# RWKV-7 recurrence in a two-layer decoder: a tile's two heads as row halves, products that alternate among the array's quarters, the inverse one turn a step

## The chip, the cores and the metric

One core of one Trainium2 chip runs the whole program. The metric is the time of one execution on the device, in microseconds (us). TensorE (PE) multiplies, VectorE (DVE), ScalarE (ACT) and GpSimd (POOL) work on tiles, SyncE (SP) and POOL issue the DMA transfers.

## What is computed

A trunk of two layers on 256 tokens of width 2048 in float32: a gated linear recurrence (RG-LRU) with its MLP, then an RWKV-7 time mixing with its MLP. The change touches only the time mixing. Cut to what matters:

```python
def rwkv7_time_mix(x, ...):
    r, k, v = ...                      # three 2048x2048 projections of shifted x
    decay, a, g = ...                  # low-rank projections
    kk = heads(k * k_k); kk = kk / max(norm(kk), 1e-12)      # 32 heads of 64
    k_mod = k * (1.0 + (a - 1.0) * k_a)
    def step(state, inp):              # state: 64x64 for each head
        r_t, w_t, k_t, v_t, kk_t, a_t = inp
        sa = einsum('bhij,bhj->bhi', state, kk_t)
        state = (state * w_t[:, :, None, :]
                 - sa[..., None] * (kk_t * a_t)[:, :, None, :]
                 + v_t[..., None] * k_t[:, :, None, :])
        y_t = einsum('bhij,bhj->bhi', state, r_t)
        return state, y_t
    _, y = lax.scan(step, state0, xs)
    y = group_norm(y) * ln_g + ln_b + bonus(r, k_mod, v)
    return (y * g) @ w_out
```

## The kernel before, in words

**Tiles.** The 256 tokens are four chunks (c = 0 to 3) of T = 64. The 2048 features are 16 tiles of 128 partitions, and one tile f holds two heads (e = 0, 1) of 64. Two tiles make a pair p (0 to 7), eight tiles a half hf (0, 1), four tiles a group s of a half. The scan over tokens is rewritten by chunks: inside a chunk a 64x64 triangular matrix of each head and chunk is inverted, and from chunk to chunk a 64x64 state is carried.

**Projections.** `linear` (from L196) streams a weight matrix in chunks of 128x1024 (`raw`). ACT casts a chunk to `hi` (L153), DVE subtracts to get `lo` (L154), two chunks ahead (AHEAD = 2). PE then multiplies each 128x128 block three times (`mm3`, L189 to L191). After every fourth k it calls `between`, which steps generators ("lanes") at a rate given per projection, so that the recurrence's work is mixed into the stream of the projections k, r, v and rwo (the output projection; PSUM tiles `ps_k`, `ps_r`, `ps_v`, `ps_rwo`). A scheduler then sets the order on each engine from these steps, with some reordering by readiness. In the profile k runs until about 1155 us, r from 1155 to 1300, v from 1300 to 1473, rwo from 1473 to about 1632.

**Preparation.** Lane `prep` (L686) runs once a tile while r and v are multiplied: low-rank products `pu`, squared norms `pn` (L725, 4 matmuls of 2 columns a tile), a scan for the decays, the tiles `BK` and `ZR` (L742 to L749), the products of all pairs of tokens of a chunk `sc`, their mask (`SC`, L766), and transposes of BK into `BKT`. Then POOL stores SC, ZR and BKT to scratch in DRAM (`scD` L772, `zrD` L773, `bkD` L777) with 1, 1 and half a transfer a tile; it also stores and reloads the pair's r (`rD` L783, `rs` L680). All of these stand on POOL's queue in the order of the program.

**Inverse.** Lane `diag`: `diagonal(hf)` (L801) loads the 32x32 diagonal blocks of the triangles of eight tiles from scD, and inverts 128 x 8 of them at once on DVE, row by row: 31 turns of a multiplication (L832) and an addition (L836) of up to 128x256 elements. It yields twice a turn for half 0 and once for half 1. `inverse(hf)` (L845) transposes the result on DVE (L854 XD, L856 XR) and makes the off-diagonal block in 32x32 products on PE: `pq` (L870), a copy to `G` on ACT, `px` (L876), a copy into `XT`; first for one row half (bh = 0), then for the other.

**Core.** Lanes core0 and core1: `core(hf, s)` (L929) goes through the four chunks for the four tiles of its group. With each chunk it makes `pw` = old state times Z (L973) plus the triangle's upper part times V (L977), scales it to `Ws` on DVE (L981), `pu` = inverse times Ws (L988), copies it to `U` on ACT, then `pS` (L997) for the new state `Sb` (DVE L1001, L1003), and y in the other row half of pw (L1007), which ACT copies out (L1011). The two row halves of a tile of tokens are two chunks: with chunk parity `par`, V lies in the rows of its parity (`pk`) and Ws and U in the other rows (`pb`), so that L997 and L1007 contract V and U in one matmul of 128 rows. The state Sb is a 128x128 block diagonal of two heads, so L973 is a 128x128 matmul. All eight matmuls of a step of L977, and of L988, lie in the same quarter of the array:

```python
            for f, e, o in es:                                   # L976
                pe.matmul(
                    pw[pb, f, o], lhsT=SC[pk, f, e, zo : zo + T], rhs=VU[pk, f, o],
                    start=c == 0 and f + e == 0, stop=True, skip_group_check=True,
                )
```

**Around it.** `centred` makes V without its mean (`pc`, L917, 4 matmuls of 128x128 a pair), `output` turns Y back with 4 transposes a pair (`pyt`, L1048) and adds the bonus and gate. Every fp32 matmul stands twice in the records, as two instructions.

## Time and profile before

| | |
|---|---|
| median of 3 runs | 2364.64 us (2361.79 to 2365.59) |
| the profiled execution | 2363.43 us |
| its span, first to last instruction | 2361.7 us |
| mean granted TensorE clock | 0.990 of 2.4 GHz |
| busy, share of the span | PE 98%, PE's weight loads 89%, DVE 66%, ACT 52%, POOL 5% |

The profile is one execution. The times of its rows are added up against 2363.43 us; the median of the runs is 1.2 us above. Busy PE time is not useful work by itself: matmuls overlap, so what a matmul costs is read from the distance of starts within a run of like ones, not from its length. A row of the timeline that says x32 is a run of 32 instructions, with the time from the first start to the last end.

### The profile page before, as it was taken

The numbers are of one execution on the slowest core, as the hardware profiler recorded it, in microseconds if no ns is written. First come the engines' busy times: TensorE is split into PE (matmuls) and PEld (weight loads), VectorE is DVE, ScalarE is ACT, GpSimd is POOL, SyncE is SP. The second block draws the span as 40 slices with busy tenths as digits, with TensorE's granted clock in tenths as the row PEclk, the third lists the DMA queues.
The fourth block names the chain that finished last, engine by engine and source line by source line (L and its number), as shares of the span: only waits on it lengthen the run. The fifth ranks groups of instructions, "written<-read, shape, count | busy, mean of one in ns | idle before, by whom it ended". The sixth has DMA issues, their size and how long they took to land.

```text
span 2361.7 us, 39553 instructions
## 1 busy us (share of the span) xinstructions
PE 2317.3 (98%) x16040; PEld 2095.0 (89%) x16040; DVE 1563.8 (66%) x2024; ACT 1236.2 (52%) x1664; POOL 119.7 (5%) x218
## 2 busy tenths in 40 slices
PE   8999999999999999989999999999999999999998
PEld 8999888888888888879989899998888888888887
DVE  7777666666656666678788948467666566666565
ACT  7787544444444444568676544345444444444454
POOL 0000000000000000000023231200000000000000
PEclk9999999999999999989999999899999999999999
DMA  6655655555565565655678877645656655655654
GB/s 225 194 167 170 191 183 189 189 190 190 188 188 189 187 194 188 205 170 197 205 252 278 281 240 244 203 148 181 190 190 188 188 189 190 190 188 188 188 187 143
DMA packets 132135, 463.12 MB, mean 196 GB/s; under 512 B 15728, under 2 KB 15984, under 8 KB 131952
## 3 DMA queue, kind: packets, MB, share of 16 engines
q1 hardware_dynamic: 115568, 405.54, 53.9%
q0 software_dynamic: 15808, 52.96, 7.0%
q8 instruction: 125, 2.05, 0.4%
q10 hardware_dynamic: 576, 2.10, 0.2%
q14 instruction: 58, 0.48, 0.1%
HBM read 430.13 MB, written 30.41 MB: 195 GB/s over the span
## 4 chain that ended last, share of the span: by engine, by line
PE 89%; DVE 3%; DMA 2%; issue 2%; ACT 2%; POOL 1%; SPq 0%; ACTq 0%; POOLq 0%; DVEq 0%
PE ps_up L234 20%; PE ps_dn L234 20%; PE ps_up L236 10%; PE ps_dn L236 10%; PE ps_rgout L234 2%; PE ps_rwo L234 1%; PE ps_gate L191 1%; PE ps_gate L190 1%; PE ps_gate L189 1%; PE ps_k L191 1%; PE ps_k L190 1%; PE ps_k L189 1%; PE ps_rgout L236 1%; PE ps_rec L191 1%; PE ps_rec L190 1%
## 5 line engine op out<-in xcount | busy, mean ns | idle before, releaser
L154 DVE TENSOR_TENSOR lo<-raw,hi 128x1024 fp32r<-128x1024 f32 x736 | 900.2, 1224 | 660.9 <-ACT hi L153 660.1
L153 ACT CAST hi<-raw 128x1024 fp32r<-128x1024 f32 x736 | 772.7, 1050 | 942.8 <-PE ps_dn L234 365.5
L234 PE MATMUL ps_up<-mx,hi 128*128 128x512 f32 x2048 | 644.3, 396 | 0.0
L234 PE MATMUL ps_dn<-ao,hi 128*128 128x512 f32 x1984 | 623.5, 396 | 0.0
L236 PEld LDWEIGHTS ps_up<-mx,lo 128*128 128x128 f32 x2048 | 384.7, 188 | 90.9
L236 PEld LDWEIGHTS ps_dn<-ao,lo 128*128 128x128 f32 x1984 | 372.7, 188 | 88.1
L236 PE MATMUL ps_up<-mx,lo 128*128 128x256 f32 x2048 | 402.4, 278 | 0.0
L236 PE MATMUL ps_dn<-ao,lo 128*128 128x256 f32 x1984 | 389.8, 278 | 0.0
L234 PEld LDWEIGHTS ps_up<-mx,hi 128*128 128x128 f32 x2048 | 312.1, 189 | 0.2
L234 PEld LDWEIGHTS ps_dn<-ao,hi 128*128 128x128 f32 x1984 | 302.0, 189 | 0.0
L189 PE MATMUL ps_rec<-rgx,hi 128*128 128x256 f32 x256 | 73.8, 288 | 8.7 <-ACT hi L153 8.7
L234 PE MATMUL ps_rgout<-rgy,hi 128*128 128x512 f32 x256 | 80.4, 396 | 0.6 <-ACT hi L153 0.6
L189 PE MATMUL ps_k<-xk,hi 128*128 128x256 f32 x256 | 74.4, 291 | 4.3 <-ACT xk L153 3.0
L191 PE MATMUL ps_k<-xk,lo 128*128 128x256 f32 x256 | 74.3, 291 | 2.6 <-DVE lo L154 2.6
L191 PE MATMUL ps_v<-xv,lo 128*128 128x256 f32 x256 | 73.8, 288 | 2.2 <-DVE lo L154 2.2
L189 PE MATMUL ps_v<-xv,hi 128*128 128x256 f32 x256 | 74.9, 292 | 0.0
L191 PE MATMUL ps_rec<-rgx,lo 128*128 128x256 f32 x256 | 73.9, 289 | 1.0 <-DVE lo L154 1.0
L190 PE MATMUL ps_k<-xk,hi 128*128 128x256 f32 x256 | 74.3, 290 | 0.4 <-DVE xk L154 0.4
L190 PE MATMUL ps_v<-xv,hi 128*128 128x256 f32 x256 | 73.8, 288 | 0.0
L190 PE MATMUL ps_rec<-rgx,hi 128*128 128x256 f32 x256 | 73.8, 288 | 0.0
L189 PE MATMUL ps_r<-xr,hi 128*128 128x256 f32 x256 | 73.5, 287 | 0.0
L191 PE MATMUL ps_r<-xr,lo 128*128 128x256 f32 x256 | 72.9, 285 | 0.0
(336 smaller groups left out, 3552.0 us busy)
## 6 DMA issues: line engine op xcount, KB each, us to landing
raw<-in_up SPq DMA_DIRECT2D x256, 512.0 KB, 3.9
raw<-in_down SPq DMA_DIRECT2D x256, 512.0 KB, 3.8
raw<-in_rkv SPq DMA_DIRECT2D x96, 512.0 KB, 4.6
raw<-in_w_in SPq DMA_DIRECT2D x64, 512.0 KB, 4.3
raw<-in_rg_out SPq DMA_DIRECT2D x32, 512.0 KB, 3.6
raw<-in_rw_out SPq DMA_DIRECT2D x32, 512.0 KB, 3.7
scD<-SC POOLq DMA_DIRECT2D x16, 512.0 KB, 5.9
SCc<-scD POOLq DMA_DIRECT2D x16, 512.0 KB, 6.8
```

The source lines that it names most:

```text
L153: nc.scalar.copy(out=hi, in_=src)
L154: dve.tensor_tensor(out=lo, in0=src, in1=hi.bitcast(F32), op=ALU.subtract)
L189: pe.matmul(ps, lhsT=whi, rhs=xhl[:, 0:S], start=start, stop=False, **kw)
L190: pe.matmul(ps, lhsT=whi, rhs=xhl[:, S : 2 * S], start=False, stop=False, **kw)
L191: pe.matmul(ps, lhsT=wlo, rhs=xhl[:, 0:S], start=False, stop=stop, **kw)
L234: pe.matmul(ps, lhsT=hi[:, o], rhs=ops[m], start=m == 0, **kw)
L236: pe.matmul(ps[:, 0], lhsT=lo[:, o], rhs=ops[m][:, 0:S], start=False, **kw)
```

## The change

**Row halves.** The two row halves of every tile become the tile's two heads (e), for all four chunks alike, and no longer two chunks. `smask` becomes one mask, scD holds for each head its triangle's parts k = 0, 1 in that head's rows, vtD becomes [P, NCH, 8, T], and the tiles SC, BKT, V, U, Ws and Y are indexed by chunk. In SC and BKT as PE makes them a row half is one kind of product (k), in scD and bkD it is a head (e); so a tile's store of SC is four transfers (one for each k and e) and that of BKT four, all on POOL's queue; the loads of the diagonal blocks are 6 transfers for a half instead of 12.

**Products.** The 128-row products of V and U together are split into one of V and one of U, the 128x128 products with the block-diagonal state into 64x64 ones, and all of core's products go through the eight (f, e) in turn with `own` = the head's rows and `other` = the other rows. `pw`, `pu` and `pS` go into own, `py` into other, so that successive matmuls lie in different quarters. py, y's accumulator, is begun with V before the state is there. Ws, U, Sb and Y are one operation of 128x256 each; the memset of Sb is gone. `centred` makes 16 matmuls of 64 columns a pair, `pn` 8 a tile instead of 4, `output` 16 products of 64x64 with the identity instead of 4 transposes.

**Inverse.** pq and px hold both row halves in one tile and alternate between them. `diagonal` yields once a turn for both halves.

```diff
@@ prep
-        pn = pp.tile([P, 2, 2], F32, tag="sm", name=f"pn_{f}")
+        pn = pp.tile([P, NCH], F32, tag="sm", name=f"pn_{f}")
         for c in range(NCH):
-            pe.matmul(pn[parts(1 - c % 2), :, c // 2], lhsT=sq[:, c * T : (c + 1) * T], rhs=heads2, start=True, stop=True)
+            for e in range(2):
+                pe.matmul(
+                    pn[parts(e), c : c + 1], lhsT=sq[:, c * T : (c + 1) * T], rhs=ones_h[:, T * e : T * e + 1],
+                    start=True, stop=True,
+                )
...
-        nc.gpsimd.dma_start(out=scD[hf][:, :, f8], in_=SC)
+        for k in range(2):
+            for e in range(2):
+                nc.gpsimd.dma_start(out=scD[hf][parts(e), :, f8, k], in_=SC[parts(k), :, e])
+                nc.gpsimd.dma_start(out=bkD[hf][parts(e), :, f8, T * k : T * k + T], in_=BKT[parts(k), :, parts(e)])
         nc.gpsimd.dma_start(out=zrD[hf][:, :, f8, :], in_=ZR[:, j].rearrange("p c s t -> p c (s t)"))
         prepared[p] += 1
         if prepared[p] == 2:
             nc.gpsimd.dma_start(out=tD[p], in_=rs)
-            nc.gpsimd.dma_start(out=bkD[hf][:, :, f8 - 1 : f8 + 1, :], in_=BKT)
@@ diagonal
-            for _ in range(2 - hf):
-                yield
+            yield
@@ inverse
-        for bh in range(2):
-            q0, q1 = slice(64 * bh, 64 * bh + 32), slice(64 * bh + 32, 64 * bh + 64)
-            pq = pp.tile([P, 32, 32], F32, tag="big", name=f"pq_{hf}_{bh}")
-            for n in range(32):
-                pe.matmul(pq[q1, n, :], lhsT=A01[q0, n, :], rhs=XR[q0, n, :], start=True, stop=True)
+        pq = pp.tile([P, 32, 32], F32, tag="big", name=f"pq_{hf}")
+        px = pp.tile([P, 32, 32], F32, tag="big", name=f"px_{hf}")
+        qs = [(slice(64 * bh, 64 * bh + 32), slice(64 * bh + 32, 64 * bh + 64)) for bh in range(2)]
+        for part in range(4):
+            for n in range(8 * part, 8 * part + 8):
+                for q0, q1 in qs:
+                    pe.matmul(pq[q1, n, :], lhsT=A01[q0, n, :], rhs=XR[q0, n, :], start=True, stop=True)
+            if part % 2:
+                yield
...
@@ core
+            es = [(f, e, parts(e), parts(1 - e)) for f in range(4) for e in range(2)]
+            for f, e, own, other in es:
+                pe.matmul(pw[own, f], lhsT=SC[own, f, 0, T:], rhs=V[own, f], start=f == 0, stop=c == 0, **kw)
+                pe.matmul(py[other, f], lhsT=SC[own, f, 0, 0:T], rhs=V[own, f], start=f == 0, stop=False, **kw)
+            if not last:
+                for f, e, own, other in es:
+                    pe.matmul(pS[own, f], lhsT=BKT[own, f, 0], rhs=V[own, f], start=f == 0, stop=False, **kw)
             if c > 0:
-                for f in range(4):
-                    pe.matmul(
-                        pw[:, f, :], lhsT=ZR[:, f, :], rhs=Sb[:, f, :], start=f == 0, stop=False, skip_group_check=True
-                    )
...
+                for f, e, own, other in es:
+                    pe.matmul(pw[own, f], lhsT=ZR[own, f, 1], rhs=Sb[own, f], start=False, stop=True, **kw)
+                    pe.matmul(py[other, f], lhsT=ZR[own, f, 0], rhs=Sb[own, f], start=False, stop=False, **kw)
+            dve.tensor_tensor(
+                out=Ws, in0=pw, in1=rho[:, c, g].unsqueeze(2).to_broadcast([P, 4, T]), op=ALU.mult
+            )
...
+            for f, e, own, other in es:
+                if not last:
+                    pe.matmul(pS[own, f], lhsT=BKT[own, f, 1], rhs=U[own, f], start=False, stop=True, **kw)
+                pe.matmul(py[other, f], lhsT=SC[own, f, 1, 0:T], rhs=U[own, f], start=False, stop=True, **kw)
@@ output
-                for cc in range(2):
-                    pe.transpose(pn[:, j, cc * P : (cc + 1) * P], Y[:, cc, 2 * (p % 2) + j, :], ident)
+                for c in range(NCH):
+                    for e in range(2):
+                        o = parts(1 - e)
+                        pe.matmul(
+                            pn[parts(e), j, c * T : (c + 1) * T], lhsT=Y[o, c, 2 * (p % 2) + j, :], rhs=ident[o, o],
+                            start=True, stop=True,
+                        )
```

The order on the engines moves at three places. On PE, at the start of the last chunk of a core (names are tile, then half, chunk, group; the row's end gives rows x columns of the weights and how many matmuls follow each other), the products before were:

```order
L973 MATMUL pwu_0_3_1_14833<-Sb_0_1_14332,VZ_0_3_1_14686 128x128 x4
L977 MATMUL pwu_0_3_1_14833<-VZ_0_3_1_14686,SCc_0_3_1_14684 64x64 x8
L973 MATMUL pwu_0_3_0_14862<-Sb_0_0_14359,VZ_0_3_0_14722 128x128 x4
L977 MATMUL pwu_0_3_0_14862<-VZ_0_3_0_14722,SCc_0_3_0_14720 64x64 x8
L988 MATMUL pwu_0_3_1_14833<-WB_0_3_1_14832,XT_0_13999 64x64 x8
L190 MATMUL ps_v_6_14639<-xv_5_13144,hi_442_14641 128x256
L191 MATMUL ps_v_6_14639<-xv_5_13144,lo_442_14642 128x256
L988 MATMUL pwu_0_3_0_14862<-WB_0_3_0_14861,XT_0_13999 64x64 x8
```

Now, at the same step of the cores of half 1:

```order
L188 MATMUL ps_rwo0_3_16601<-ry_1_14892,lo_454_16347 128x256
L982 MATMUL pwu_1_3_0_16621<-VZ_1_3_0_16416,SCc_1_3_0_16415 64x64
L983 MATMUL pwu_1_3_0_16621<-VZ_1_3_0_16416,SCc_1_3_0_16415 64x64
...
L983 MATMUL pwu_1_3_0_16621<-VZ_1_3_0_16416,SCc_1_3_0_16415 64x64
L989 MATMUL pwu_1_3_0_16621<-Sb_1_0_15986,VZ_1_3_0_16416 64x64
L990 MATMUL pwu_1_3_0_16621<-Sb_1_0_15986,VZ_1_3_0_16416 64x64
...
L990 MATMUL pwu_1_3_0_16621<-Sb_1_0_15986,VZ_1_3_0_16416 64x64
L982 MATMUL pwu_1_3_1_16656<-VZ_1_3_1_16466,SCc_1_3_1_16465 64x64
L983 MATMUL pwu_1_3_1_16656<-VZ_1_3_1_16466,SCc_1_3_1_16465 64x64
```

Runs of four or eight like products in one place become pairs that alternate, L982 into the own rows and L983 into the other, and the products with V stand ahead of those with the state. The first pq of half 0 moves too: it stood behind pc_3, the fourth pair of v, and stands ahead of pc_0, the first. In v, core(0, 0) ran together with core(0, 1), step by step; now it runs ahead of it by itself, with 2 to 11 rows of `ps_v` between some of its steps.

On DVE, in the last part of the projection r and the first of v, one turn of the inverse of half 0 (L832 and L836 before) stood between several operations of `prep` and the splits L154:

```order
L832 TENSOR_TENSOR tm_0_2_12824<-AD_0_12675,X_0_12595 128x112
L154 TENSOR_TENSOR lo_415_13064<-raw_415_13062,hi_415_13063 128x1024
L742 TENSOR_TENSOR BK_10_12829<-kk_10_12800,Pi_10_12798 128x2x128
L743 TENSOR_TENSOR BK_10_12829<-tha_10_12786,Pi_10_12798 128x2x2x64
L747 SCALAR_TENSOR_TENSOR ZR_5_12752<-ks_5_12723,V_69,Pd_10_12797 128x2x128
L748 TENSOR_TENSOR ZR_5_12752<-rs_5_12725,Pd_10_12797 128x2x2x64
L836 TENSOR_TENSOR X_0_12595<-X_0_12595,tm_0_2_12824 128x28x4
L749 SCALAR_TENSOR_TENSOR rs_5_12725<-rs_5_12725,V_69,tha_10_12786 128x256
L832 TENSOR_TENSOR tm_0_4_12900<-AD_0_12675,X_0_12595 128x135
L154 TENSOR_TENSOR xv_4_13136<-xm_2_4_13137,xv_4_13136 128x2x256
L836 TENSOR_TENSOR X_0_12595<-X_0_12595,tm_0_4_12900 128x27x5
L154 TENSOR_TENSOR xv_5_13144<-xm_2_5_13145,xv_5_13144 128x2x256
```

Now (L828 and L832 are the same two operations, L151 the split) every operation of the inverse alternates with one other:

```order
L748 TENSOR_TENSOR ZR_5_12847<-rs_5_12820,Pd_10_12901 128x4x64
L828 TENSOR_TENSOR tm_0_6_12980<-AD_0_12766,X_0_12679 128x175
L749 SCALAR_TENSOR_TENSOR rs_5_12820<-rs_5_12820,V_69,tha_10_12884 128x256
L832 TENSOR_TENSOR X_0_12679<-X_0_12679,tm_0_6_12980 128x25x7
L151 TENSOR_TENSOR lo_415_13204<-raw_415_13202,hi_415_13203 128x1024
L828 TENSOR_TENSOR tm_0_6_12980<-AD_0_12766,X_0_12679 128x192
L766 TENSOR_TENSOR SC_10_13032<-sc_10_13018,K128_71 128x4x128
L832 TENSOR_TENSOR X_0_12679<-X_0_12679,tm_0_6_12980 128x24x8
L766 TENSOR_TENSOR SC_10_13032<-sc_10_13018,K128_71 128x4x128
L828 TENSOR_TENSOR tm_0_8_13015<-AD_0_12766,X_0_12679 128x207
L726 TENSOR_SCALAR SS_1_3561<-pn_11_13098 128x4
L832 TENSOR_TENSOR X_0_12679<-X_0_12679,tm_0_8_13015 128x23x9
```

Between the splits of the weight chunks 415 and 416 stand 26 of them instead of 13, and until the split of chunk 421 62 instead of 34, with the two transposes XD and XR behind them; from chunk 434 on the count is equal again.

On POOL, for the fifth tile's stores and the pair's r that follows, the queue held:

```order
L772 DMA scD_0_3550<-SC_4_12135 512x1x256
L783 DMA rD_3_3529<-rs0_3_12206 128x512
L773 DMA zrD_0_3551<-ZR_2_11986 512x1x128
L776 DMA tD_2_3544<-rs_2_11962 128x512
L731 MEMSET Pd_7_12428 128x4
L680 DMA rs_3_12213<-rD_3_3529 128x512
L777 DMA bkD_0_3552<-BKT_2_11987 384x1x256
```

Now the stores are four and four:

```order
L773 DMA bkD_0_3552<-BKT_2_12023 192x1x64 x4
L772 DMA scD_0_3550<-SC_4_12181 256x1x128 x4
L783 DMA rD_3_3529<-rs0_3_12263 128x512
L774 DMA zrD_0_3551<-ZR_2_12022 512x1x128
L777 DMA tD_2_3544<-rs_2_11998 128x512
L731 MEMSET Pd_7_12506 128x4
L677 DMA rs_3_12270<-rD_3_3529 128x512
L773 DMA bkD_0_3552<-BKT_2_12023 192x1x64
L772 DMA scD_0_3550<-SC_5_12324 256x1x128 x2
L773 DMA bkD_0_3552<-BKT_2_12023 192x1x64
L772 DMA scD_0_3550<-SC_5_12324 256x1x128
```

The load of the next pair's r (L680, now L677) stands behind seven more issues here, and over the whole preparation POOL issues 64 stores of SC and 64 of BKT instead of 16 and 8.

## Rows read from the trace of the kernel before

**Rows 1.** The page: the span, and the chain that ended last by engine.

```profile
span 2361.7 us, 39553 instructions
...
PE 89%; DVE 3%; DMA 2%; issue 2%; ACT 2%; POOL 1%; SPq 0%; ACTq 0%; POOLq 0%; DVEq 0%
```

**Rows 2.** Windows: stretch, length, busy PE PEld DVE ACT POOL, clock, DMA share, GB/s.

```profile
1300.00:1347.00 47.00, 42.77 (x382) 40.55 (x381) 46.12 (x100) 28.33 (x57) 13.63 (x24) 0.96 0.80 267
...
1395.00:1472.80 77.80, 77.61 (x861) 72.25 (x860) 60.46 (x110) 33.81 (x51) 18.19 (x33) 1.00 0.74 239
...
1486.00:1503.00 17.00, 16.50 (x305) 16.00 (x306) 5.68 (x6) 8.79 (x9) 0.57 (x1) 0.82 0.75 242
...
1504.00:1516.00 12.00, 12.00 (x75) 10.75 (x74) 3.30 (x4) 2.20 (x3) 0.00 (x0) 0.50 0.15 45
```

**Rows 3.** Groups on DVE, 1300 to 1329 and (the transpose) 1347 to 1395 us.

```profile
L832 DVE TENSOR_TENSOR tm<-AD,X 128x255 f32<-128x255 f32 (+7 forms) x9 | 3.6, 403 | 0.0
L836 DVE TENSOR_TENSOR X<-X,tm 128x255 f32<-128x255 f32 (+7 forms) x9 | 3.6, 403 | 0.0
...
L856 DVE STREAM_TRANSPOSE XR<-X 128x1024 f32<-128x1024 f32 x1 | 2.2, 2231 | 0.0
```

**Rows 4.** Groups on POOL, 1155 to 1640 us: busy us, mean ns, idle before.

```profile
L772 POOL DMA_DIRECT2D scD<-SC x16 | 11.8, 738 | 20.7 <-DVE SC L766 19.3 <-DVE SS L726 0.6 <-DVE X L836 0.6
```

**Rows 5.** One line's view, POOL's loads of r (L680): what they and their users wait for.

```profile
L680 POOL DMA_DIRECT2D rs<-rD x8: 542/552/561, 1179.6 to 1309.5; - x8
...
  DMA rD<-rs: 15.9, 7
...
  DVE ZR L748: 5.2, 2
```

**Rows 6.** Timeline of POOL: start us, us, what [idle before].

```profile
1286.28 0.54 POOL L680 DMA_DIRECT2D rs<-rD  x1 [3.58 <-DMA rD<-rs]
...
1298.01 0.54 POOL L680 DMA_DIRECT2D rs<-rD  x1 [4.79 <-DMA rD<-rs]
```

**Rows 7.** Groups on PE by form, whole span: the count of one step's products.

```profile
L977 PE MATMUL pwu<-VZ,SCc 64*64 64x64 f32 x256 | 19.9, 233 | 0.0
```

**Rows 8.** Timeline of PE: runs of like matmuls, from a first start to a last end.

```profile
1486.50 2.21 PE L870 MATMUL pq<-XR,A 32*32 32x32 f32 x64 [1.49 <-DVE XR L856]
...
1523.79 2.08 PE L988 MATMUL pwu<-WB,XT 64*64 64x64 f32 x29
1525.80 0.69 PE L997 MATMUL pS<-VZ,WB 128*64 128x64 f32 x16
...
1539.92 1.16 PE L973 MATMUL pwu<-Sb,VZ 128*128 128x128 f32 x8
...
1547.74 0.28 PE L191 MATMUL ps_rwo<-ry,lo 128*128 128x256 f32 x1
1547.95 2.08 PE L1007 MATMUL pwu<-VZ,SCc 128*64 128x64 f32 x32
1549.96 0.39 PE L189 MATMUL ps_rwo<-ry,hi 128*128 128x256 f32 x1
1550.18 0.28 PE L190 MATMUL ps_rwo<-ry,hi 128*128 128x256 f32 x1
1550.30 0.28 PE L191 MATMUL ps_rwo<-ry,lo 128*128 128x256 f32 x1
```

**Rows 9.** Timeline of PE: single starts where products of two quarters stand mixed.

```profile
1494.16 0.19 PE L870 MATMUL pq<-XR,A 32*32 32x32 f32 x1
1494.16 0.19 PE L876 MATMUL px<-XD,G 32*32 32x32 f32 x1
...
1523.68 0.22 PE L988 MATMUL pwu<-WB,XT 64*64 64x64 f32 x1
1523.68 0.22 PE L977 MATMUL pwu<-VZ,SCc 64*64 64x64 f32 x1
1523.73 0.22 PE L988 MATMUL pwu<-WB,XT 64*64 64x64 f32 x1
```

More of the change, by code (lines that the diff above doesn't have):

```diff
@@ L969, in core @@
-            pw, pu = pwu[:, 0], pwu[:, 1]
-            es = [(f, e, slice(64 * e, 64 * e + 64)) for f in range(4) for e in range(2)]
-            if c > 0:
-                for f in range(4):
-                    pe.matmul(
-                        pw[:, f, :], lhsT=ZR[:, f, :], rhs=Sb[:, f, :], start=f == 0, stop=False, skip_group_check=True
-                    )
-            for f, e, o in es:
-                pe.matmul(
-                    pw[pb, f, o], lhsT=SC[pk, f, e, zo : zo + T], rhs=VU[pk, f, o],
-                    start=c == 0 and f + e == 0, stop=True, skip_group_check=True,
-                )
+            last = c == NCH - 1
@@ new lines, in core @@
+            SC, V, U, ZR = now
+            WB = t_(f"WB_{hf}_{c}_{s}", [P, 8 * P])
+            Ws = WB[:, 0 : 2 * P].rearrange("p (f i) -> p f i", i=T)
+            BKT = WB[:, 4 * P :].rearrange("p (f k j) -> p f k j", k=2, j=T)
+            if not last:
+                nc.gpsimd.dma_start(out=WB[:, 4 * P :], in_=bkD[hf][:, c, g])
+                now = load(c + 1)
+            pwu = pp.tile([P, 2, 2, 4, T], F32, tag="big", name=f"pwu_{hf}_{c}_{s}")
+            pw, pu, py = pwu[:, 0, 0], pwu[:, 0, 1], pwu[:, 1, 0]
@@ L993, in core @@
             yield
-            if c < NCH - 1:
-                pS = pp.tile([P, 4, T], F32, tag="sm", name=f"pS_{hf}_{c}_{s}")
-                for f, e, o in es:
-                    pe.matmul(pS[o, f, :], lhsT=BKT[:, f, o], rhs=VU[:, f, o], start=True, stop=True)
-                for o in (slice(0, 64), slice(64, 128)):
-                    St, new = Sb[o, :, o], pS[o]
-                    if c > 0:
-                        dve.tensor_tensor(out=St, in0=St, in1=new, op=ALU.add)
-                        new = St
-                    dve.tensor_tensor(
-                        out=St, in0=new, in1=PT[hf][o, g, c : c + 1].to_broadcast([64, 4, T]), op=ALU.mult
-                    )
@@ L1006, in core @@
-            for f, e, o in es:
-                pe.matmul(
-                    pw[pk, f, o], lhsT=SC[:, f, e, ro : ro + T], rhs=VU[:, f, o],
-                    start=c == 0 and f + e == 0, stop=True, skip_group_check=True,
+            for f, e, own, other in es:
+                if not last:
+                    pe.matmul(pS[own, f], lhsT=BKT[own, f, 1], rhs=U[own, f], start=False, stop=True, **kw)
+                pe.matmul(py[other, f], lhsT=SC[own, f, 1, 0:T], rhs=U[own, f], start=False, stop=True, **kw)
@@ L1010, in core @@
+            if not last:
+                new = pS
+                if c > 0:
+                    dve.tensor_tensor(out=Sb, in0=Sb, in1=pS, op=ALU.add)
+                    new = Sb
+                dve.tensor_tensor(
+                    out=Sb, in0=new, in1=PT[hf][:, g, c : c + 1].to_broadcast([P, 4, T]), op=ALU.mult
                 )
-            nc.scalar.copy(out=Y[pk, cc], in_=pw[pk])
+            nc.scalar.copy(out=Y[:, c], in_=py)
             yield
```

131 lines of the change are left out of this document (58 added, 73 removed).

## The prediction

> **What bounds the kernel now.** I read the page first, for the bound: the chain of work that ended last lies on PE for 89% of the span, and no other engine has more than 3% [rows 1]. So a change pays what it takes off PE's stream, and costs what it makes PE wait for. Then the windows, to see where that does not hold. In v from 1395 us on PE is busy 77.6 of 77.8 us, so there DVE, ACT and POOL have slack and only PE's own work counts. From 1300 to 1347 it is the other way round: DVE is busy 46.1 of 47 us and PE stands still for 4.2 us. And in rwo the granted clock falls: 0.82 from 1486 to 1503, then 0.50 (the 1.2 GHz level) from 1504 to 1516 [rows 2]. Then the timeline of PE, for the pace of each kind of small product, since a group's mean is a length and not what the product costs. The runs shown have a median 1.2 us above the profiled execution's 2363.4 us; the sum below is made against the latter. About 0.2%, 4.7 us, is what a measurement of this kernel can tell from no change.
>
> **Paces.** All in ns from start to start. A run of 29 instructions of 64x64 in one quarter takes 2.08 us, one of 32 of 128x64 from 1547.95 to 1549.96 takes 2.01: some 62, I use 61, the mean of several such runs being near it. Sixteen of L997, whose columns alternate between two halves, take 0.69: (0.69 - 0.22) / 15 = 31. Eight of 128x128 take 1.16: (1.16 - 0.28) / 7 = 126, and I use 120 since the last end is long. 32x32 in one quarter: 2.21 for 64, 32 after the last length is taken off [rows 8]. Where L988 and L977, which read different row halves, stand mixed, two start at 1523.68 and the next at 1523.73; of pq and px two start at the same hundredth [rows 9]. So two quarters overlap. That four do is not shown anywhere.
>
> **The parts.**
>
> (a) *Core's products.* Before: L977, L988 and L1007 with 256 instructions each ([rows 7] for the first; one product for each of 32 heads and 4 chunks, two instructions a product, so the others have as many), 768 x 61 = 46.8 us; L997 192 x 31 = 6.0; L973 96 x 120 = 11.5. Together 64.3. After, by the diff: pS with V and pu go to two quarters in turn, 192 + 256 = 448 instructions x 31 = 13.9. The others (pw and py with V 512, with the state 384, pS and py with U 448) go to four in turn: 1344. Their pace is not in the trace: at best half of 31, 15; at worst 31, as two in turn. I take 22, in the middle, as the two quarters of [rows 9] come near the half but share no row half: 29.6. Sum 43.5, so **-21 us** (-30 to -9). All of it lies on PE, in stretches where PE is full.
> The Trainium skill ("TensorE: Matmul & The Clock Gate", section "Wait — 56ns, not 53.3ns?") states a floor of about 25 ns between starts however small a matmul is. [Rows 9] have two starts within one hundredth of a microsecond, which a floor between single starts does not allow, though one on their mean would hold at 1523.68. By it the 1344 would take 33.6 us, the part -17, and the whole 2361.
>
> (b) *Inverse.* 512 instructions of 32x32 (128 products each of pq and px, two instructions each) at 32 = 16.4 us. In two quarters in turn 16 at best, 32 at worst; I take 24: **-4** (-8 to 0).
>
> (c) *More small matmuls.* Output: 32 transposes' instructions x 120 = 3.8 become 256 x 31 = 7.9, +4 (if 61: +12). centred: 64 x 120 = 7.7 become 256 x 31 = 7.9, nothing. pn doubles, 128 more of 2 columns, at some 30 each +3.8, but mostly while PE waits in r: +1. **+5**.
>
> (d) *Changes of tile form.* Before L1007's run the next start comes 0.21 us on, behind it 0.22, where linear's own matmuls follow each other at 0.12 [rows 8]: some 0.1 to 0.15 a change. The order has 91 such changes from the start of v to the end of rwo before, 124 after: 33 x 0.13 = **+4**.
>
> (e) *The slow clock.* It follows on pq and px of half 1, which stand almost alone on PE from 1486.5 on [rows 8]; lost are 0.18 x 17 + 0.5 x 12 = 9 us [rows 2]. In the new order they lie inside v among `ps_v`, shorter, and half 0's lay there in v at clock 1.00 already [rows 2]. I take the loss as gone, with the 1.5 us that pq waited for XR [rows 8]: **-10.5** (-12 to 0, if core's own runs bring the clock down in their turn).
>
> (f) *The inverse's turns in r and v.* One turn a yield puts 28 more operations of L832 and L836 before the split of chunk 421: at 0.33 (0.40 for wide ones [rows 3], later ones are narrower) 9.3 us, and two transposes at 2.2 [rows 3]: 13.7 us of DVE work earlier, in a stretch where DVE has 0.9 us free of 47. PE cannot multiply before the split is there. Two chunks stand ready, so about 2.5 us are covered: **+11** (5 to 14). That DVE does less later gives nothing back, PE being full there [rows 2].
>
> (g) *Stores.* 104 more POOL issues at 0.74 [rows 4]. Seven of them, 5.2 us, stand straight ahead of each load of r; POOL waits there 2.3 us on average anyway (15.9 in 7) [rows 5], so the load goes out 2.9 later. ZR waited for it in two cases [rows 5]: 6 us, of which I take **+4**, as they fall partly into (f)'s lateness (0 to 25).
>
> (h) *Hand-overs.* core(0, 0) now runs by itself. It has 12 hand-overs to DVE and ACT and back, each some 0.8 (an operation of 0.40 [rows 3] and a matmul's 0.22 on each side [rows 9]); the `ps_v` rows in between cover about half: **+5** (0 to 10). Core's fewer DVE and ACT operations count nothing, as PE is the full engine there.
>
> **Sum**: -21 - 4 + 5 + 4 - 10.5 + 11 + 4 + 5 = -6.5, so 2357.
>
> **The rivals.**
>
> *Four quarters at once.* Products at 15, inverse at 16, and the stores hidden by POOL's idle time: -30 - 8 + 5 + 4 - 10.5 + 11 + 0 + 5 = -23.5, 2340. For it speaks the near-simultaneous pairs [rows 9]; against it that two quarters of L997, which share both row halves, come at 31 and not closer. Chance 0.19.
>
> *POOL's queue sets the pace of preparation.* Thirteen more issues a pair are 9.6 us; with about 5.6 before (seven or eight issues by the order) and the wait of 2.3 for r's store, a pair needs 17.5 us of POOL. The loads of r stand 18.6 us apart on average [rows 5], so it would just do, but the last ones only 11.7 [rows 6]: from the point where pairs follow closer than 17.5 us, POOL decides. Two such pairs lose 5.8 each: 2357 + 12 = 2369. More if one issue of the smaller runs costs more than 0.74, or if half 1's diagonal loads then come late as well (another 9.6). For it speaks that POOL's issues are one after the other; against it, its 0.74 were measured on larger stores. Chance 0.24.
> The Trainium skill ("DMA: Bandwidth & Descriptors", section "Specifications") says that transfers under 512 bytes are read, modified and written back. The new stores of BKT go in runs of 256 bytes; no row here shows such a store, so the trace neither bears it out nor speaks against it, and it gives no price.
>
> *Two at a time is all.* The 1344 start no closer than 31, the inverse stays at 32: (a) -9, (b) 0, the rest as above: 2373. For it speaks that no row shows a mean under 25 for 64 columns; against it pq and px in pairs [rows 9]. Here the change does not do what its alternation is for. Chance 0.15.
>
> **The numbers.** The forecast has 0.42; within its own bounds (2350 to 2364) about two thirds are faster by over 0.2%: 0.28, the rest 0.14 the same. With four at once, faster is 0.28 + 0.19 = 0.47. POOL's case gives 0.22 slower and 0.02 the same, two at a time 0.15 slower: slower 0.37, same 0.16. The range goes from 2335, a little under four at once, to 2384, POOL's case with late diagonal loads: 2335 to 2384.
>
> **What would show it.** (a): runs of L982 and L983 in turn with starts under 25 ns apart, 31 would be the third rival; PE busy less between 1400 and 1590. (b): pq and px of 64 in about 1.6 us. (e): clock 1.00 in rwo; a fall elsewhere takes up to 9 back. (f): a wait of PE for the split `lo` between 1300 and 1350 that is longer by about 11. (g): DVE's ZR waiting for rs over 5.2 us in sum; over 20 means that POOL decides. (d) and (h): short idle times at hand-overs in core(0, 0). I am wrong altogether if v begins over 10 us later than 1300, or if the products' pace is not under 31.

## The result, and the profile after

The changed kernel takes 2383.54 us (median of 4 runs, 2378.23 to 2387.81), the kernel before beside it 2365.11 us (2361.79 to 2366.65): a ratio of 1.0079, 95% interval 1.0054 to 1.0103. It is 18 us slower, where 6.5 us faster was forecast; the time lies just under the upper end of the range, 2384, and on the other side of no change. The profiled execution took 2378.23 us, the shortest of the four, so the profiles show 14.8 of the 18 us; what follows compares its span with that before.

The page after, to be read beside [rows 1]: PE's work fell by 14.7 us (it was 2317.3 us before), and the span grew by 14.8. So the products were made cheaper, and some 30 us more of PE's time stand empty.

```profile
span 2376.5 us, 42213 instructions
...
PE 2302.6 (97%) x17320; PEld 2075.2 (87%) x17320; DVE 1550.8 (65%) x2004; ACT 1230.7 (52%) x1664; POOL 172.3 (7%) x306
...
PE 89%; DMA 3%; DVE 3%; issue 2%; ACT 2%; POOL 1%; SPq 0%; ACTq 0%; DVEq 0%; POOLq 0%
```

The windows after (columns as in [rows 2]):

```profile
1300.00:1347.00 47.00, 36.99 (x328) 34.74 (x326) 45.91 (x110) 29.79 (x60) 26.55 (x48) 0.78 0.73 209
1310.00:1330.00 20.00, 12.64 (x83) 11.70 (x83) 20.00 (x46) 10.68 (x25) 14.48 (x26) 0.50 0.67 192
...
1395.00:1472.80 77.80, 70.62 (x1388) 61.95 (x1388) 57.24 (x114) 32.31 (x52) 18.46 (x32) 0.98 0.76 251
...
1508.00:1552.00 44.00, 32.32 (x767) 29.88 (x766) 11.98 (x20) 8.76 (x15) 12.41 (x23) 0.84 0.68 232
```

After the change v runs from 1309 to 1501 us and rwo from there (1300 and 1473 before). Three stretches answer to [rows 2]. From 1300 on DVE is full as before, but PE idles 10.0 of 47 us instead of 4.2, and from 1310 to 1330 it gets the clock of 0.50. In v from 1395 on, where PE was full, it is idle for 7.2 of 77.8 us. In rwo the slow clock has not gone: between 1508 and 1552 PE idles 11.7 us, and the clock is 0.84. What PE waited for, from 1155 to 1660 us (us in total, times, longest):

```profile
PE pS L986 <- DMA WB<-bkD: 7.5, 3, 3.9
PE pwu L982 <- issue: 5.2, 2, 4.9
PE pu L186 <- ACT l L150: 4.5, 3, 2.3
PE ps_v L188 <- DVE lo L151: 4.3, 1, 4.3
PE ps_v L186 <- ACT vs L913: 4.1, 1, 4.1
```

The first two are core's: the load of BKT, and waits for which the view names nothing ("issue"). The longest of these, 4.9 us at the start of half 1's core, is by POOL's timeline a wait for V. POOL could issue V's load only when V's own store to DRAM had landed, and the load took 3.9 us to land:

```profile
1510.32 0.57 POOL L953 DMA_DIRECT2D VZ<-vtD  x1 [4.76 <-DMA vtD<-vt]
...
1514.27 0.24 PE L982 MATMUL pwu<-VZ,SCc 64*64 64x64 f32 x1 [4.88 <-issue]
```

Before, the 32x32 products of half 1's inverse lay between the last pair of v and that core (from 1486.5 on [rows 8]); now they run inside v, from 1483 to 1496 us. The third wait is for the low-rank weights of preparation, the fourth for the split of a weight chunk on DVE. The fifth is a copy of v that stands on ACT behind the cast of a weight chunk (1392.79), which had waited 1.9 us for its load.

**By stages.** The first pair of v was copied out at 1326.15 us before and at 1348.31 after (ACT's copy `vs`): 22.2 us lost by then. From there to the end of the first part of rwo (1585.9 and 1600.7) 7.4 us were won back. The sum had +15 for the first, (f) and (g), and -21.5 for the second, the rest. The windows of the second stretch, two before and two after:

```profile
1326.15:1473.00 146.85, 146.39 (x1629) 139.61 (x1630) 104.22 (x179) 68.38 (x96) 42.14 (x71) 1.00 0.79 256
1473.00:1585.90 112.90, 111.19 (x1249) 104.49 (x1249) 64.34 (x99) 45.84 (x62) 16.78 (x30) 0.91 0.55 175
...
1348.31:1501.00 152.69, 141.39 (x2491) 129.95 (x2484) 93.79 (x156) 69.21 (x100) 44.50 (x75) 0.99 0.75 244
1501.00:1600.70 99.70, 87.94 (x1498) 81.73 (x1497) 48.38 (x68) 33.98 (x54) 14.21 (x26) 0.93 0.58 193
```

PE idles 23.1 us in it instead of 2.2. The slow clock takes about 8.5 us instead of 10.2, an estimate: what the clock lacks to 1, times the length of each window.

**The paces.** The timeline of PE shows what the alternation does:

```profile
1347.92 1.83 PE L868 MATMUL pq<-XR,A 32*32 32x32 f32 x104 [0.48 <-PE sc L759]
...
1400.35 0.27 PE L1003 MATMUL pS<-VZ,WB 64*64 64x64 f32 x1 [0.24 <-ACT VZ L999]
1400.36 0.27 PE L1004 MATMUL pwu<-VZ,SCc 64*64 64x64 f32 x1
1400.36 0.27 PE L1003 MATMUL pS<-VZ,WB 64*64 64x64 f32 x1
...
1400.86 0.22 PE L982 MATMUL pwu<-VZ,SCc 64*64 64x64 f32 x1
...
1430.86 0.68 PE L986 MATMUL pS<-VZ,WB 64*64 64x64 f32 x16 [0.19 <-ACT yv L1064]
...
1470.79 1.15 PE L1052 MATMUL pyt<-K,Y 64*64 64x64 f32 x32
```

The 32 instructions of L1003 and L1004 start between 1400.35 and 1400.86: 16 ns each, where one quarter gave 61 [rows 8]. Those that go to two quarters, L986, come at 31, as before L997, and so does pyt (1.15 us for 32). pq in two quarters: (1.83 - 0.2) / 103 = 16 ns, half of [rows 8].

### The profile page after: what moved, and what is told of

The parts are those of the page before. It is cut to its first block, busy times and chain, and to the rows that moved or that the text cites. A ratio compares the mean times of both kernels' runs of the same rounds, so it can differ in the third digit from the quotient of the medians.

```text
span 2376.5 us, 42213 instructions
## 1 busy us (share of the span) xinstructions
PE 2302.6 (97%) x17320; PEld 2075.2 (87%) x17320; DVE 1550.8 (65%) x2004; ACT 1230.7 (52%) x1664; POOL 172.3 (7%) x306
## 4 chain that ended last, share of the span: by engine, by line
PE 89%; DMA 3%; DVE 3%; issue 2%; ACT 2%; POOL 1%; SPq 0%; ACTq 0%; DVEq 0%; POOLq 0%
PE ps_up L231 20%; PE ps_dn L231 19%; PE ps_up L233 10%; PE ps_dn L233 10%; PE ps_rgout L231 2%; PE ps_rwo L231 1%; PE ps_gate L188 1%; PE ps_gate L187 1%; PE ps_gate L186 1%; PE ps_k L188 1%; PE ps_k L187 1%; PE ps_k L186 1%; PE ps_rgout L233 1%; PE ps_rec L188 1%; PE ps_rec L187 1%
## 5 line engine op out<-in xcount | busy, mean ns | idle before, releaser
L151 DVE TENSOR_TENSOR lo<-raw,hi 128x1024 fp32r<-128x1024 f32 x736 | 900.0, 1223 | 689.8 <-ACT hi L150 688.7
L186 PE MATMUL ps_rec<-rgx,hi 128*128 128x256 f32 x256 | 73.2, 286 | 9.0 <-ACT hi L150 9.0
L186 PE MATMUL ps_r<-xr,hi 128*128 128x256 f32 x256 | 75.1, 294 | 0.2 <-ACT rs L782 0.2
L187 PE MATMUL ps_r<-xr,hi 128*128 128x256 f32 x256 | 73.9, 289 | 0.0
```

Source lines behind the costliest of these rows:

```text
L151: dve.tensor_tensor(out=lo, in0=src, in1=hi.bitcast(F32), op=ALU.subtract)
L186: pe.matmul(ps, lhsT=whi, rhs=xhl[:, 0:S], start=start, stop=False, **kw)
L187: pe.matmul(ps, lhsT=whi, rhs=xhl[:, S : 2 * S], start=False, stop=False, **kw)
```

## The experiments

Each ratio is of the kernel to the kernel before, run beside it on the same chip.

**The turns, alone and undone.** Two runs: the changed kernel with the yields of half 0 as before, and the kernel before with the yields changed.

```diff
-            yield
+            for _ in range(2 - hf):
+                yield
```

> The changed kernel with one thing undone: the inverse of half 0 yields twice a turn again. Theory 1 (the turns: one turn a step puts 13.7 us of DVE work into a stretch where DVE is full, PE waits for splits and then runs at a clock of 0.50 from 1310 to 1330, and the cores of half 0 fall apart so that each stands alone): the wait for the splits goes, the first pair of v is done some 14 us earlier than in the changed kernel, the two cores of half 0 run together, and the time is 2360 to 2367. Theory 2 (POOL's split stores and core's loads from DRAM are what costs): the time stays above 2375, since neither is touched. If both count: 2367 to 2375.

> The kernel before with only the inverse's yields changed to one a turn for half 0; products, stores and layout as before. Theory 1: slower by 14 us or more, 2379 or above, with PE waiting for splits between 1300 and 1350 and a granted clock of 0.50 behind it. Theory 2: the turns alone cost little, 2362 to 2368.

Measured: 2369.92 us (1.0028, interval 1.0017 to 1.0038) with two yields in the changed kernel, 13.6 us less than with one; 2377.42 us (1.0061, 1.0049 to 1.0073) with one yield in the kernel before, 13.3 us more than with two. The window of the kernel before, and of that last run:

```profile
1300.00:1350.00 50.00, 45.77 (x407) 43.55 (x406) 48.88 (x108) 29.39 (x58) 16.05 (x28) 0.97 0.82 272
...
1300.00:1350.00 50.00, 39.23 (x443) 37.21 (x444) 47.44 (x102) 30.41 (x55) 14.19 (x24) 0.83 0.68 209
```

With no other part of the change PE idles 10.8 us there instead of 4.2, and the clock is 0.83 instead of 0.97. So of the 13.3 us some 6.5 are waits and, by estimate, 7 the slow clock (0.14 x 50). The turn a step costs 13 to 14 us by itself, in either kernel. By the expectations the first run lies where both theories count (2367 to 2375), and the second just under theory 1's 2379; at 2370 the rest of the change is no gain either. One sign failed: with two yields the changed kernel has its first pair of v at 1343.54, only 4.8 us earlier and not 14, as v's first matmul comes at 1315.5 there, later than the 1308.7 of the changed kernel. The runs on l2raw below come back to that.

**Cores together.** The cores of a half wait for all four pairs of their half.

```diff
-        while hf not in XTs or any(4 * hf + p not in v_done for p in range(2 * s, 2 * s + 2)):
+        while hf not in XTs or any(4 * hf + p not in v_done for p in range(4)):
```

> The changed kernel, where the cores of a half wait for all four pairs of v of their half, so that both groups run step by step together as before; the one-turn yields stay. Theory 1 with the part that lonely cores expose each hand-over and load: the idle times of PE at L982, L983 and L986 between 1395 and 1460 (some 6 us in the changed kernel) shrink to under 2 us, time 2372 to 2379. Rival: the loads of core are late by themselves (buffers come free only behind L1004), so running together changes nothing: 2381 to 2387.

Measured: 2380.81 us (1.0067, 1.0054 to 1.0081), 2.7 less than the changed kernel, whose interval overlaps, and just under the rival's range. From 1395 to 1460 us PE still waits 8.8 us for V and BKT at L982 and L986, where under 2 were expected. That core(0, 0) stands alone is not the main cost.

**Split stores alone.** The kernel before, with its stores cut into 4 + 4 a tile.

```diff
-        nc.gpsimd.dma_start(out=scD[hf][:, :, f8], in_=SC)
+        for k in range(2):
+            for e in range(2):
+                nc.gpsimd.dma_start(out=scD[hf][parts(k), :, f8, e], in_=SC[parts(k), :, e])
+                nc.gpsimd.dma_start(
+                    out=bkD[hf][parts(k), :, f8, T * e : T * e + T], in_=BKT[parts(k), :, j, T * e : T * e + T]
+                )
...
```

> The kernel before with its stores of SC and BKT cut into four transfers each a tile (row halves to the same row halves, so the numbers are the same), 104 more issues on POOL and runs of 512 and 256 bytes; nothing else. Theory 2: the pairs of r come later by about 8 us by 1290, as in the changed kernel, where r's fifth pair was done 8.9 us later with the clock at 0.90 to 0.95 between 1190 and 1260 instead of 0.95 to 1.00: 2370 to 2376. Theory 1 alone: the stores are hidden, 2363 to 2368. In between, 2368 to 2370, leaves it open.

Measured: 2374.69 us (1.0037, 1.0023 to 1.005). By the expectation's numbers theory 2. But the profile of this run puts only 2.8 us of it into r (v begins at 1303.0 instead of 1300.2); 3.4 more come in v, and 5.7 in the first part of rwo, where the granted clock is lower (0.79, against 0.87 in the same window of the kernel before):

```profile
1480.00:1560.00 80.00, 78.26 (x935) 73.95 (x933) 34.50 (x59) 25.01 (x32) 16.79 (x30) 0.79 0.61 192
```

So the stores by themselves cost some 6 us by lateness up to rwo, a little over the 4 of (g), and the slow stretch that rwo had already became longer behind them. At the first pair of v the turns alone come 15.0 us late (its copy at 1341.17) and the stores alone 7.0 (1333.13), together about the 22.2 of the changed kernel.

**Fewer issues, other pieces.** The changed kernel with its eight stores a tile joined to four; the same with two yields; and the kernel before with its stores cut by 32 rows, so that there are as many issues but no smaller runs.

```diff
+        for k in range(2):
+            nc.gpsimd.dma_start(
+                out=scD[hf][:, :, f8, k].rearrange("(e p) c s -> p c e s", e=2), in_=SC[parts(k)]
+            )
...
```

```diff
+        for k in range(4):
+            r4 = slice(32 * k, 32 * k + 32)
+            nc.gpsimd.dma_start(out=scD[hf][r4, :, f8], in_=SC[r4])
+            nc.gpsimd.dma_start(out=bkD[hf][r4, :, f8], in_=BKT[r4, :, j])
...
```

> The changed kernel with its eight stores a tile of SC and BKT joined to four (both heads in one transfer; runs of 512 and 256 bytes stay): 64 instead of 128 issues on POOL. If the count of issues on POOL's queue is what the stores cost (10.6 us in the kernel before with stores cut up), half of it comes back: 2374 to 2380. If it is the small runs, nothing comes back: 2381 to 2386.

> The changed kernel with both undone as far as possible: two yields a turn for half 0 and the joined stores. If turns (13.6 us by the first pair of runs) and issues on POOL (half of 10.6) add up: 2369.9 - 5 = 2362 to 2367, about as the kernel before. If the small runs cost, not the issues: 2368 to 2372. A gain over the kernel before of more than 5 us (under 2359) would mean that the products' gain had been hidden by the stores alone.

> The kernel before with its stores of SC and BKT cut into four transfers each a tile by 32 rows: the same 104 more issues on POOL as in the run with split stores, but runs of 1024 and 512 bytes. If the issues are what costs: as that run, 2371 to 2377. If the small runs (512 and 256 bytes) were what cost there: 2363 to 2367.

Measured: 2387.81 us (1.0101, 1.0083 to 1.0118), 2370.94 us (1.003, 1.0017 to 1.0043) and 2393.73 us (1.0127, 1.0104 to 1.0149). Half the issues bring nothing back, in either form. All three expectations that priced the count of issues missed; the second run lies in the range for small runs (2368 to 2372), the other two above all their ranges. The Trainium skill's rule on transfers under 512 bytes ("DMA: Bandwidth & Descriptors", section "Specifications") would make the cut by rows the cheaper one, with its runs of 512 bytes and more; at 2393.73 against 2374.69 us it does not show here. But the times of these two runs cannot settle it, since the order differs too: the cut by rows also puts the loads of the low-rank weights up to five weight chunks later on SP, which led to the runs on SP's queue below. The times from issue to landing speak more directly (the last number of a row, in us), split stores first, then the cut by rows:

```profile
scD<-SC POOLq DMA_DIRECT2D x64, 128.0 KB, 4.3
bkD<-BKT POOLq DMA_DIRECT2D x64, 48.0 KB, 3.9
...
scD<-SC POOLq DMA_DIRECT2D x64, 128.0 KB, 3.9
bkD<-BKT POOLq DMA_DIRECT2D x64, 48.0 KB, 4.4
```

BKT's stores land in 3.9 us in runs of 256 bytes and in 4.4 in runs of 512, SC's in 4.3 in runs of 512 and 3.9 in runs of 1024. So no price of small runs is seen, and what the split stores cost beyond their lateness stays open.

**No alternation.** The kernel with joined stores and two yields, with core's products one quarter after another.

```diff
-            es = [(f, e, parts(e), parts(1 - e)) for f in range(4) for e in range(2)]
+            es = [(f, e, parts(e), parts(1 - e)) for e in range(2) for f in range(4)]
```

and each pair of own and other products in two loops instead of one.

> As the run with turns and stores undone, but core's products one quarter after another (all eight tiles' products of a kind head by head, own and other apart) instead of in turn. Theory: starts 61 ns apart instead of 16, so the 1792 instructions of core take 1792 x 61 = 109 us instead of some 35 us; what lies on PE's path shows as 40 to 75 us more: 2400 to 2440. Rival: hand-overs and loads, not products, bound the core, so that slower products fill time in which PE waited anyway: under 2380.

Measured: 2390.55 us (1.011, 1.0091 to 1.0129), 19.6 us over its twin and between the two expectations. The products did not go back to 61 ns. Of the 32 instructions from 1417.02 on the last starts at 1418.34:

```profile
1417.02 0.79 PE L987 MATMUL pwu<-VZ,SCc 64*64 64x64 f32 x13
1417.60 0.27 PE L989 MATMUL pwu<-VZ,SCc 64*64 64x64 f32 x1
...
1417.82 0.74 PE L989 MATMUL pwu<-VZ,SCc 64*64 64x64 f32 x13
```

That is 43 ns on the mean: in this order the quarter changes after every eight instructions, and starts of L989 come between the last ones of L987. By estimate core's 1792 instructions take 77 us at this pace instead of 35, so some 42 more and not 74, of which about half shows in the time. Part of the rest falls where PE waits otherwise. From the first pair of v to the end of the first part of rwo the twin and this run have:

```profile
1353.60:1602.90 249.30, 230.25 (x4037) 215.19 (x4038) 156.28 (x257) 106.46 (x159) 57.84 (x95) 0.97 0.70 230
...
1348.00:1604.90 256.90, 249.03 (x3940) 235.13 (x3939) 150.37 (x251) 103.36 (x155) 57.64 (x95) 0.98 0.65 215
```

PE idles 7.9 us with the slower products and 19.1 with the faster ones. (The twin's profile is of its longest execution, 2380.19 us; the run with two yields alone idles 17.2 there.)

**r's reload, and the state's products.** On the kernel with two yields: rs loaded on SP; pS with V moved behind pu; both; and rs on SP in the kernel before as the control.

```diff
-        nc.gpsimd.dma_start(out=rs, in_=rD[p])
+        nc.sync.dma_start(out=rs, in_=rD[p])
```

```diff
+            if not last:
+                for f, e, own, other in es:
+                    pe.matmul(pS[own, f], lhsT=BKT[own, f, 0], rhs=V[own, f], start=f == 0, stop=False, **kw)
             nc.scalar.copy(out=U, in_=pu)
```

(the same three lines are gone from their place ahead of the state's products)

> As the run with two yields (2369.9 us), but the reload of the pair's r (rs) is issued on SP's queue instead of POOL's, so that it no longer stands behind the stores. Theory: the split stores cost because the loads of r queue behind them on POOL; then ZR's waits for rs and the late pairs of r go, and 5 to 10 us come back: 2360 to 2365. Rival: preparation is a ring of tight dependences (stores, mask, splits on DVE) and not this one load: 2368 to 2373. If SP, which then waits for r's own store, holds up the weight chunks behind it: above 2374.

> As the run with two yields (2369.9 us), but the products of pS with V stand behind pu instead of ahead of the state's products. Theory: PE waits at L986 (7.5 us in the changed kernel, 5.5 in the run with two yields) for BKT's load, which was only issued at the chunk's begin, and the granted clock falls behind it in rwo (0.66 and 0.72 from 1510 to 1530 in the run with two yields); later they find BKT loaded and fill PE while ACT copies U: 5 to 9 us, 2361 to 2365. Rival: the wait moves to the next load of the chunk (SC, V, ZR): 2367 to 2372.

> Two yields, the reload of r on SP and pS with V behind pu, all three. If both theories hold the gains add up: 2352 to 2360, faster than the kernel before. If neither: 2368 to 2372.

> The kernel before with only the reload of r on SP's queue: the control. If the load's place behind stores matters only since the stores were split, no change: 2361 to 2367. If it held up preparation already (ZR waited 5.2 us for rs): 2357 to 2361. If SP's waits hold up weight chunks: above 2368.

Measured: 2369.2 us (1.0012, 1.0001 to 1.0022), 2365.76 us (1.0001, 0.9992 to 1.001), 2364.61 us (0.9997, 0.9989 to 1.0006), control 2364.93 us (1.0, 0.9988 to 1.0012). Moving pS with V brings about 4 us, a little less than its theory's 5 to 9: ahead of the state's products it waited for a load that is issued at the chunk's own begin, and held up what stood behind it on PE. r's reload on SP is worth 1 to 4 us by the ratios, which is the rival's range, and nothing in the kernel before. The two together came out between their two expectations.

**The low-rank weights' place on SP.** Before, the load `l2raw` of pair 1 follows one weight chunk; in the changed order it follows two, of which the second waits 7 us for its buffer. SP's timelines, before and after:

```profile
1190.85 0.33 SPq L178 DMA_DIRECT2D raw<-in_rkv  x1
1191.27 0.38 SPq L676 DMA_DIRECT2D l2raw<-in_lora  x1
```

```profile
1189.87 7.10 SPq L175 DMA_DIRECT2D raw<-in_rkv  x2
1197.07 0.49 SPq L673 DMA_DIRECT2D l2raw<-in_lora  x1
```

ACT, then `pu`, then PE wait for it. ACT's waits for it between 1155 and 1310 us, before and after (us in total, times, longest):

```profile
ACT l L153 <- DMA l2raw<-in_lora: 4.0, 1, 4.0
...
ACT l L150 <- DMA l2raw<-in_lora: 13.0, 4, 5.5
```

The load is asked for two steps of `prep` earlier, in the changed kernel as it is, in the one with two yields, r's reload on SP and pS later, and in the kernel before (with r's reload on SP).

```diff
...
+        if j == 0:
+            raw_load(p + 1)
         dve.tensor_tensor_scan(thw, cmask, thw, 0.0, op0=ALU.mult, op1=ALU.add)
```

> The changed kernel with one load moved: each pair's low-rank weights (l2raw, on SP's queue) are asked for before the decays' scan of the pair ahead, some two weight chunks earlier. Theory: in the changed order l2raw of pairs 1, 3 and 5 stands one weight chunk later on SP than before (behind raw_397, 404 and 416 instead of 396, 403 and 415), each such chunk waits up to 7 us for its buffer, so ACT, then pu, then PE wait (13.0 us of waits of ACT for l2raw, 4.5 of PE for l), and the granted clock falls behind each: 6 to 10 us come back, 2373 to 2378. Rival: the split stores or DVE hold preparation back, l2raw only comes last by chance: 2381 to 2386.

> The same move of l2raw in the kernel with two yields, r's reload on SP and pS with V later (2364.6 us). There v begins at 1316, 16 us later than in the kernel before. Theory: 6 to 12 us come back, 2352 to 2359, now faster than the kernel before. Rival: 2362 to 2367.

> The control: the kernel before with r's reload on SP and l2raw asked for early, none of the change. If the early l2raw only mends what the changed order broke, no gain: 2362 to 2368. If it helps any order of preparation: 2354 to 2361.

Measured: 2382.31 us (1.0069, 1.0055 to 1.0082), 2353.74 us (0.9948, 0.9935 to 0.996) and control 2363.48 us (0.9995, 0.9985 to 1.0006). In the kernel with two yields it brings 10.9 us, and v's first matmul moves from 1316.3 to 1302.0 us; the kernel before has nothing to gain from it. In the changed kernel as it is it brings 1.2, inside the spread, and so lies with the rival: v begins 6 us earlier there too (1302.7), but its first pair only 2.1 (1346.25), while DVE is busy 36.6 of the 38 us from 1308 to 1346 with the inverse's turns among its work. From 1200 to 1250 us, where pairs 1 to 3 are prepared, PE's idle time shrinks from 7.3 us to 2.5 and the clock rises; in the kernel with two yields, without the early load and with it:

```profile
1200.00:1250.00 50.00, 42.66 (x402) 40.38 (x402) 37.06 (x70) 31.61 (x67) 28.27 (x51) 0.93 0.81 248
```

```profile
1200.00:1250.00 50.00, 47.46 (x462) 44.94 (x461) 40.05 (x77) 33.46 (x71) 32.14 (x57) 0.97 0.90 290
```

**Loads or hand-overs in core.** Three runs. On the kernel with two yields, r's reload on SP and pS later, each core loads its triangles once and uses the first chunk's for all four (12 of 16 loads left out, so that the later chunks compute with the first one's triangles). On that with the early l2raw as well, first only the three quarters of SC that core reads are loaded; then, with all of SC, there is one more yield behind Ws and one behind U, so that `ps_v` or `ps_rwo` stand between core's steps.

```diff
-            SC = x_(f"SCc_{hf}_{c}_{s}", [P, 4, 2, P])
+            SC = once.get("SC")
+            if SC is None:
+                SC = once["SC"] = x_(f"SCc_{hf}_{c}_{s}", [P, 4, 2, P])
+                nc.gpsimd.dma_start(out=SC, in_=scD[hf][:, c, g])
...
```

```diff
-            nc.gpsimd.dma_start(out=SC, in_=scD[hf][:, c, g])
+            nc.gpsimd.dma_start(
+                out=SC.rearrange("p f k t -> p f (k t)")[:, :, 0 : 3 * T],
+                in_=scD[hf][:, c, g].rearrange("p f k t -> p f (k t)")[:, :, 0 : 3 * T],
+            )
```

```diff
...
             nc.scalar.copy(out=U, in_=pu)
+            yield
             yield
```

> The kernel with two yields, r's reload on SP and pS with V later (2364.6 us), but each core loads its triangles SC for the first chunk only and uses them for all four; this leaves out 12 of 16 loads of 512 KB, and the later chunks compute with the first one's triangles. Theory: core's products, at 16 ns a start, are now faster than core's own loads (some 2 MB a chunk of two cores, with DMA at a share of 0.9 to 1.0 where PE idles), so PE's idle time in core (8.9 us of 60 from 1400 on, 6.8 of 50 from 1500 on) and the slow clock behind it shrink to a half or less: 2350 to 2358. Rival: the hand-overs to DVE and ACT in PE's fixed order make the idle time, whatever is loaded: 2361 to 2367.

> The kernel with l2raw early, two yields, r's reload on SP and pS with V later, which also loads only the three quarters of SC that core reads (384 instead of 512 KB a load, 768-byte runs). Theory of loads: 2 to 4 us under the kernel with l2raw early. Rival (hand-overs): no difference from it within 2 us.

> The best so far (l2raw early, two yields, r's reload on SP, pS with V later: 2353.7 us) with one more yield behind Ws and one behind U in core, so that twelve more matmuls of v or rwo stand between core's steps. Theory: PE, which goes through its order, stands still at core's hand-overs and loads (some 12 us in 1400 to 1460 and 1500 to 1560) and the clock falls behind it (0.94 in both); with more of v and rwo in between both shrink, the products' gain shows: 2335 to 2347. Rival: core only ends later and rwo then waits for its y: 2352 to 2360.

Measured: 2360.33 us (0.9975, 0.9964 to 0.9987), 4.3 less than its twin, between the two expectations; 2353.35 us (0.9954, 0.9941 to 0.9968), no difference from 2353.74, as the rival of hand-overs had it; 2352.35 us (0.9948, 0.9936 to 0.9959), 1.4 less, inside the spread, so spreading missed its 2335 to 2347. The windows of the last, from 1400 and from 1500 us:

```profile
1400.00:1460.00 60.00, 54.13 (x1183) 48.95 (x1182) 42.72 (x93) 18.32 (x31) 13.09 (x24) 1.00 0.82 270
1500.00:1560.00 60.00, 56.35 (x1120) 52.41 (x1117) 30.13 (x44) 21.01 (x36) 8.63 (x16) 0.97 0.63 214
```

PE still idles 9.5 us in these two, against 11.5 without the spreading, at a clock near 1.00. Leaving the triangles out takes the idle time of the two windows from 15.6 us to 10.4, not to a half, so loads and hand-overs share it; how they divide stays open.

## Why the prediction was wrong

**(a), (b): the direction right, the size too small.** The four quarters run at 16 ns, not 22: 448 x 31 + 1344 x 16 = 35 us instead of 64, so -29; the rival with four at once had the pace right, and *two at a time is all* is refuted. The inverse's 16 ns make (b) -8. The floor of about 25 ns that the Trainium skill gives ("TensorE: Matmul & The Clock Gate", section "Wait — 56ns, not 53.3ns?") does not hold for starts that alternate among quarters: 16 ns on the mean of 32. But (a) also took it that all of this lies where PE is full, and there it failed, as below. **(c)** was right for the transposes (31 ns).

**(f): right in size, half of it by luck.** +11 was forecast, of 13.7 us of DVE work; alone it measured 13.3, undone 13.6. But +11 was to be PE's wait for the split `lo`, and the longest such wait is 4.3 us in the changed kernel and 5.0 with the turns alone (2.2 before). Alone, the turns made some 6.5 us of waits, on several operations of DVE and not on `lo` only, and about 7 us of slow clock behind them, which the sum did not have (in the changed kernel 0.50 from 1310 to 1330).

**(g): near in size for the stores, wrong in what was looked at.** Alone the stores cost some 6 us up to rwo, where 4 were forecast, and 10.6 in all. But the sum took the order of PE, DVE and POOL and left out SP: there l2raw stood one weight chunk later, a term put at nothing, and asking for it early brings 10.9 us once the turns are undone. *POOL's queue sets the pace* forecast 2369, with a range up to the measured time. After the change POOL does issue two of r's late reloads without the idle time that [rows 6] had, and 20.2 us apart:

```profile
1292.34 0.61 POOL L677 DMA_DIRECT2D rs<-rD  x1
...
1312.58 0.59 POOL L677 DMA_DIRECT2D rs<-rD  x1
```

Yet its sign is absent: ZR waits 1.8 us for rs, and 3.4 with nothing named, where over 20 would have shown it. Half as many issues bring nothing and r's reload on another queue little, so POOL is at most a part of it.

**(h) and (e): the step that failed.** Sum: +5 and -10.5. After the first pair of v the sum, with the measured paces, would be -29 - 8 + 5 + 4 - 10.5 + 5 = -33.5; measured were -7.4, so 26 us of gain are missing. Two terms make nearly all of them. PE idles 20.9 us more in this stretch (23.1 instead of 2.2), where (h) and the 1.5 of (e) come to 3.5 more; and the slow clock takes about 2 us less, where (e) had 9 less.

(h) priced core's waits as a DVE operation and two matmuls each, and its loads at nothing. The longest waits are for DMA: BKT 7.5 us, V 4.9 at the start of half 1's core, a weight chunk behind ACT's copy 4.1. V's trip through DRAM had been covered by half 1's inverse, which the changed order moved into v; pS with V had been put ahead of a load issued at the chunk's own begin. Products of 64 us had hidden loads, as I read it; at 35 they no longer do: PE idles 17 to 19 us with the fast products and 7.9 with slower ones, and leaving out 12 triangle loads gave 4.3 us back. How much of the idle time is loads and how much hand-overs is not shown.

(e) expected the slow stretch behind half 1's pq and px to go, and it did go: they run in v now, and from 1480 to 1504 the clock is 1.00. But the slow clock came back behind the new waits:

```profile
1480.00:1504.00 24.00, 23.93 (x456) 22.76 (x456) 8.82 (x9) 12.53 (x15) 2.81 (x5) 1.00 0.56 185
...
1528.00:1538.00 10.00, 6.06 (x92) 5.58 (x82) 1.35 (x3) 1.05 (x1) 0.00 (x0) 0.51 0.57 209
```

It did not need the 32x32 products that I put it down to: neither this stretch nor that from 1310 on holds any. That (e) was gone was an argument from one case.

Taken together the change holds a gain that its order hides: with the turns undone, l2raw and pS put right and r's reload on SP it is 12 us faster than the kernel before (0.9948), and 30 us faster than as it stands in the diff.

## What to carry to other kernels

A faster product pays only as far as its operands arrive: where the products of a step were the cover for the loads of the next, price the loads' latency against the new length of the step, and look at which wait comes next in the engine's own order. A change of order is read on every queue, the one that only loads (SP) too: here a load that slipped behind one more buffer's wait cost 10.9 us. Work that is moved earlier must find a stretch where its engine has time, and where it stood before it may have covered something else, as the inverse covered V's trip through DRAM.

## What was not expected of the hardware

64x64 products that go to four quarters in turn start every 16 ns, a quarter of the 61 ns of one quarter, and 32x32 products in two quarters at 16 ns, half of 32. The granted clock fell to the 1.2 GHz level (0.50) behind idle times of PE of 1.5, 4.1, 4.9 and 2.0 us (ended at 1307.7, 1394.4, 1514.3 and 1526.9 us in the changed kernel); from 1310 to 1330 it stayed there for 20 us. Behind idle times of 2.5 and 1.6 us (ended at 1410.1 and 1440.9) it did not fall: it is 1.00 from 1400 to 1504. In the kernel before it fell at about 1497 (0.74 from 1496 to 1498, 0.50 from 1498 to 1516), after PE had been busy without a break since 1486.5, with pq and px of half 1 among its work. So neither an idle time nor its length decides alone in these traces, and what does was not settled.
